# An MLP's first half: product down with weights loaded anew for each factor, attention running on beside it

## The chip, the core and the metric

The kernel runs on one core of a Trainium2 chip. Time is device microseconds of one launch; lower is better. Engines: PE (matmul) with PEld (its weight loads), DVE, ACT, POOL, and SP, which issues most DMAs.

## What is computed

One layer on x, 2048 tokens by 1024. All is float32 outside; inside, each float32 matrix is split into a high and a low float16 part, and a product takes three matmuls (high x high, low x high, high x low).

```python
h = rmsnorm(x); proj = h @ w_in            # three head groups read h
y_a = s5_mixer(...)                        # state-space scan
y_b = diff_attention(dq, dk, dv, ...)      # 6 heads, two softmax maps each
y_c = hgrn2_mixer(cq, cf, ci, cg, ...)     # gated linear recurrence
x = x + concat(y_a, y_b, y_c) @ w_out
h = rmsnorm(x)
up = causal_conv3(h @ w_up) + conv_b; gate = h @ w_gate     # 1024 -> 2816
x = x + (gelu(up) * gate) @ w_down                          # 2816 -> 1024
return rmsnorm(x)
```

Attention, per head and block of 128 queries: scores of two maps over all keys up to the block's end, softmax of each, `w = p0 - lam * p1`, `o = w @ v`.

## The kernel before, in words

**Two streams woven.** The program is written by two generators. `fore` (`left`) writes the input projection and then attention: first query blocks 0 to 7 of all heads, then blocks 8 to 15 of all heads. The other (`right`) writes the state-space part, the recurrence, and then `phase_tail`: output projection and MLP. Each yields a number, its cost; `weave` goes on with the stream whose sum is smaller. The cost of a block of attention is its number of key blocks times a weight of the list `LW`: `LW[4]` for blocks 8 to 15. A larger weight lets attention advance more slowly beside the tail. Within the order so written, a scheduler sets the order of each engine when the kernel is built; on the chip each engine runs its instructions strictly in that order.

**The tail.** Tokens 0 to 1023 are the first half, the rest the second. `first` projects the first half (`o_pm`), normalises it, and runs 22 *up tiles* (`tile_of`, one for each 128 columns of the 2816; 84 matmuls `f_pm` each); half of these also make the float16 weights `f_w`, the other half load them. Each ends in conv, GELU and the factors `f_a`, which go to the DRAM tensors `Ad`. Then comes the *product down* of the first half (`Down`): a Strassen scheme with seven products, numbered 0 to 6, of 132 matmuls `f_pd` each. Product i multiplies a left factor `f_da` (loaded from `Ad`) by a right factor `f_dw`, which is the split of a quarter of `w_down` or of a difference of quarters. The sums go onto the rows `f_r` (loaded from `Xd`) in `put`, on DVE. Then `second` does the output projection of the second half, with product 6 inside it; the second half's up tiles and its product down end the kernel, with no attention beside them.

**Attention beside it.** For each block: scores `t_ps` (chunks of 512 keys), which DVE moves with bias and running maximum to `t_sc` (L839); exponent on ACT (L849); the difference of the maps on DVE (L861); per 512 keys four transposes `t_pt`, two copies on ACT, the low part `t_wt` on POOL (L875), and twelve matmuls `t_po` per four key blocks. After eight blocks of a head pair: a chain of thirteen tiny DVE operations for the norm, a scaling on POOL (L903), transposes of `t_y` (L910) and the split `t_yo` to `Yd`.

**Right factors before.** A right factor has four cuts of 3, 3, 3 and 2 row blocks, and `f_dw` has six buffers, so that two cuts of the next product can be written while four are in use. For products 0 to 3 the quarters are streamed through three buffers `f_dst` of at most two row blocks (`stage`), the difference made by POOL in place, the split by ACT (high) and DVE (low, L62). Ahead of product 2, `before()` writes out all of attention that is left, because the 88 KB a partition that hold the four raw quarters `f_db` (`hold`, `load`) lie where attention's buffers were. Products 4 to 6 take their differences from `f_db`, by POOL, one operation of 128x1536 or 128x1024 a cut. The second half's product down uses the same class with all quarters held.

Of the kernel before, what the change touches and what calls it, by code (L numbers as in the profile page):

```python
# [9 lines left out]
F32 = mybir.dt.float32  # L10
# [4 lines left out]
ALU = mybir.AluOpType  # L15
# [7 lines left out]
MF = DFF // 128  # L23
# [3 lines left out]
CH = 512  # L27
# [8 lines left out]
MADE = range(0, MF, 2)  # L36
LW = [6.0, 0.44, 5.0, 2.5, 0.62, 1.0]

# [1289 lines left out]
def phase_tail(K, x, Xd, Yd, Ad, w_out, norm_g, W, conv_w, conv_b, w_down, final_g, out, es,  # L1328
# [228 lines left out]
    class Down:  # L1557
# [18 lines left out]

        LOADS = ({2: (B12, B11), 3: (B22,), 4: (B21,)}, {0: (B21,), 1: (B22, B11), 2: (B12,)})

# [20 lines left out]

        def stage(self, i, st, cs=(0, 1, 2, 3)):  # L1600

            for c in cs:
                q0, n = self.cuts[c]
                w = self.room(i, c)
                for q in range(0, n, 2):
                    k = min(2, n - q)
                    b, pair, _ = self.STEPS[i]
                    fs = []
                    for b in pair or (b,):
                        f = st.tile([128, KD, 128], F32, tag="wst", name="f_dst")  # L1610
                        f = f.rearrange("p (q a) f -> p q (a f)", q=2)[:, 0:k]
                        nc.sync.dma_start(out=f, in_=self.source(b, q0 + q, k))
                        fs.append(f)
                    f = fs[0]
                    if pair:
                        add(f, f, fs[1], ALU.subtract, P)
                    K.split(w[:, 0, q:q + k], w[:, 1, q:q + k], f, WS)

# [89 lines left out]

        def run(self, rs, tp, pms, side, staged, before):


            self.rs, self.tp = rs, tp
            with ExitStack() as e1:
                pool = pooler(e1)
                st = pool("f_dst", 3) if staged > 1 else None
                self.more(pool)
                if not self.w:
                    self.ahead(st)
                with ExitStack() as e2:
                    for i in range(6):  # L1720
                        for c in range(len(self.cuts)):
                            if (i, c) not in self.a:
                                self.left(i, c)
                        if i == staged - 1 - (staged > 1):
                            before()
                            self.hold(pooler(e2)("f_db", 1, side))
                        for b in self.LOADS[self.half].get(i, ()):
                            self.load(b)
                        if i + 1 < staged:
                            self.stage(i + 1, st)  # L1730
                        else:
                            for c in range(len(self.cuts)):
                                if i + 1 == staged == 4:
                                    self.sum(3, c)
                                self.right(i + 1, c)
                        if i < 5:
                            yield from self.product(i, pms[i % len(pms)], False)
                yield from self.product(5, pms[5 % len(pms)], False)
                if self.half == 1:
                    yield from self.product(6, pms[6 % len(pms)], True)  # L1740
            self.last = self.product(6, pms[0], False)

# [146 lines left out]
    with ExitStack() as e2:  # L1889
# [6 lines left out]
        down = Down(0, pooler(el))  # L1896
        yield from down.run(total(0), tp, [pm], "left", 4, ahead)
        eh = ExitStack()
# [7 lines left out]
    eh.close()  # L1906
    yield from down.run(total(1), tp, [pd, pm], "left", 1, lambda: None)

# [116 lines left out]
```

## Time and profile before

| what | value |
|---|---|
| time, median of 3 runs | 2810.27 us (2809.77 to 2811.77) |
| profiled execution | 2806.09 us, span 2804.4 us |
| PE / DVE / ACT / POOL busy | 90% / 72% / 48% / 48% of the span |
| first up matmul, first f_pd | 1225.1 us, 1869.8 us from the span's start |
| last t_po | 1932.7 us |
| next output projection (o_pm) | from 2062.5 us |
| second half's up tiles | from 2195.7 us |

A page of the profile gives busy time by engine, slices of the span, the chain that ended last and the costliest groups of instructions. Rows of groups read: line, engine, operation, out<-in, count, busy time, mean ns of one, idle time of the engine before them and what ended it. Rows of the timeline read: start, length, engine, line, operation, and in brackets the idle time before it and who ended it. Matmuls are pipelined: a run of them shows their pace, a single one its latency.

### The profile page before, as it was taken

How to read it: one execution, taken by the hardware profiler on the slowest of the kernel's cores; microseconds unless marked ns; L12 is line 12 of the kernel's file. 1: busy time of each engine (PE TensorE's matmuls, PEld its weight loads, DVE VectorE, ACT ScalarE, POOL GpSimd, SP SyncE). 2: the span in 40 equal slices, each digit the busy share in tenths (PEclk: the TensorE clock that was granted, in tenths of full speed). 3: DMA queues.
4: the chain of work that ended last, by engine and by line, in shares of the span. 5: the costliest groups of instructions: out<-in, count | busy, mean ns of one | idle time of the engine just before them, and what ended most of it. 6: DMA issues, size and time to landing. Idle time of an engine off the chain costs nothing.

```text
span 2804.4 us, 44619 instructions
## 1 busy us (share of the span) xinstructions
PE 2528.7 (90%) x16254; PEld 1465.3 (52%) x16254; DVE 2008.0 (72%) x3904; ACT 1341.1 (48%) x2579; POOL 1347.2 (48%) x1191
## 2 busy tenths in 40 slices
PE   5998898989999998968898888879999999999998
PEld 3654546877777765444444444434444444444443
DVE  7566745788787887798888889885654855555565
ACT  5333344557665665676565456653134422222221
POOL 4788602334343443266566666642801444444180
PEclk8999998989989989989999999989999999999999
DMA  6675553232223225623444434357775655554733
GB/s 225 234 219 187 166 169 99 65 91 69 60 78 91 52 86 134 211 84 112 135 135 128 152 111 128 101 213 242 270 264 197 215 166 155 166 154 143 267 105 120
DMA packets 339500, 420.74 MB, mean 150 GB/s; under 512 B 61840, under 2 KB 217808, under 8 KB 338256
## 3 DMA queue, kind: packets, MB, share of 16 engines
q1 hardware_dynamic: 317104, 377.51, 42.8%
q10 hardware_dynamic: 22176, 40.38, 3.9%
q8 instruction: 128, 2.10, 0.3%
q14 instruction: 92, 0.75, 0.1%
HBM read 289.30 MB, written 127.93 MB: 149 GB/s over the span
## 4 chain that ended last, share of the span: by engine, by line
PE 41%; DVE 16%; issue 6%; ACT 4%; DMA 4%; POOL 4%; SPq 0%; ACTq 0%; DVEq 0%; POOLq 0%
PE f_pm L98 18%; PE f_pd L1679 10%; DVE t_sc L839 3%; PE o_pm L1394 3%; DVE t_sc L861 2%; PE g_pv L98 2%; PE g_pq L98 1%; ACT t_sc L849 1%; PE t_pt L871 1%; DVE f_t L1520 1%; PE t_ps L835 1%; DVE f_w L62 1%; DMA o_y<-Yd 1%; PE g_pl L1147 1%; PE t_po L883 1%
## 5 line engine op out<-in xcount | busy, mean ns | idle before, releaser
L98 PE MATMUL f_pm<-f_q,f_w 128*128 128x512 f16 x3696 | 857.8, 388 | 6.2 <-DVE rs_i L72 5.7
L98 PEld LDWEIGHTS <-f_w 128*128 128x128 f16 x3696 | 365.3, 100 | 493.7 <-issue 98.4
L875 POOL TENSOR_TENSOR t_wt<-t_wf,t_wt 128x512 f16<-128x512 f32 (+2 forms) x240 | 286.5, 1195 | 451.3 <-ACT t_wt L874 365.0
L1679 PE MATMUL f_pd<-f_dw,f_da 128*128 128x512 f16 x1848 | 406.9, 382 | 9.5 <-DMA f_da<-Ad 7.8
L1679 PEld LDWEIGHTS <-f_da 128*128 128x128 f16 x1848 | 181.3, 98 | 228.7 <-DMA f_da<-Ad 8.8
L849 ACT ACTIVATE t_sc<-t_sc,t_nm 128x128 f32<-128x128 f32 (+7 forms) x192 | 229.2, 1198 | 53.5 <-DVE t_nm L844 51.9
L835 PE MATMUL t_ps<-t_k,t_q 96*128 96x512 f16 (+2 forms) x480 | 170.0, 369 | 83.7 <-DVE t_mx L839 80.5
L839 DVE CUSTOM_DVE_ANT_0 t_sc<-t_ps,t_base,t_mx 128x512 f32<-128x512 f32 (+3 forms) x288 | 185.2, 643 | 36.4 <-PE t_ps L835 29.6
L873 ACT ACTIVATE t_wf<-t_pt 128x512 f32<-128x512 f32 (+2 forms) x240 | 126.7, 528 | 132.9 <-PE t_pt L871 96.1
L883 PE MATMUL t_po<-t_v,t_wt 128*128 128x64 f16 x2448 | 145.5, 198 | 37.1 <-POOL t_wt L875 32.4
L883 PEld LDWEIGHTS <-t_wt 128*128 128x128 f16 x2448 | 124.8, 101 | 94.3 <-POOL t_wt L875 48.0
L861 DVE SCALAR_TENSOR_TENSOR t_sc<-t_sc,t_a 128x1024 f32<-128x1024 f32 (+7 forms) x144 | 167.9, 1193 | 1.6
L98 PE MATMUL g_pq<-g_h,g_w 128*128 128x256 f16 x1152 | 157.3, 291 | 9.9 <-DVE g_sg L1069 7.3
L60 DVE TENSOR_TENSOR f_a<-f_t,f_a 128x512 f16<-128x512 f32 x132 | 134.8, 1027 | 39.6 <-ACT f_a L54 36.1
L98 PE MATMUL g_pv<-g_w,g_h 128*128 128x256 f16 x1152 | 151.1, 284 | 12.0 <-ACT g_w L54 8.0
L1744 POOL TENSOR_TENSOR f_k<-f_k,f_k 128x512 f32<-128x512 f32 x88 | 126.1, 1433 | 73.1 <-ACT f_k L1776 65.9
L871 PE MATMUL t_pt<-ident,t_sc 128*128 128x128 f32 x816 | 146.6, 296 | 14.6 <-ACT t_wt L874 9.4
L1744 POOL TENSOR_TENSOR f_db<-f_db 128x1536 f32<-128x1536 f32 (+1 forms) x32 | 129.2, 4073 | 61.0 <-DMA f_db<-in_w_down_dram 61.0
L1744 POOL TENSOR_TENSOR f_t<-f_t,f_t 128x512 f32<-128x512 f32 x66 | 104.3, 1594 | 108.5 <-ACT f_a L54 85.4
L1394 PE MATMUL o_pm<-o_w,o_y 128*128 128x512 f16 x624 | 145.0, 388 | 10.0 <-DMA o_y<-Yd 9.6
L54 ACT ACTIVATE f_a<-f_t 128x512 f16<-128x512 f32 x154 | 95.9, 629 | 118.1 <-POOL f_t L1744 54.9
L62 DVE SCALAR_TENSOR_TENSOR f_dw<-f_db,f_dw 128x1536 f16<-128x1536 f32 (+1 forms) x36 | 104.0, 2904 | 55.2 <-ACT f_dw L54 55.2
(328 smaller groups left out, 4856.5 us busy)
## 6 DMA issues: line engine op xcount, KB each, us to landing
f_w<-Wd SPq DMA_DIRECT2D x231, 256.0 KB, 2.7
Wd<-f_w SPq DMA_DIRECT2D x154, 256.0 KB, 2.1
Ad<-f_a ACTq DMA_DIRECT2D x154, 256.0 KB, 2.3
f_da<-Ad SPq DMA_DIRECT2D x42, 768.0 KB, 4.5
g_h<-Hd SPq DMA_DIRECT2D x24, 1024.0 KB, 6.5
f_db<-in_w_down_dram SPq DMA_DIRECT2D x24, 768.0 KB, 8.7
o_wst<-in_w_out_dram SPq DMA_DIRECT2D x32, 512.0 KB, 5.8
o_y<-Yd SPq DMA_DIRECT2D x52, 256.0 KB, 4.9
```

What stands on the lines that cost most here:

```text
L60: nc.vector.tensor_tensor(out=lo, in0=src, in1=hi, op=ALU.subtract)
L98: nc.tensor.matmul(out=out, lhsT=lhs(a, k), rhs=rhs(b, k), start=(n == 0), stop=(n == 3 * nk - 1))
L835: nc.tensor.matmul(out=ps[:, 0:k1 - k0], lhsT=qt[:, c, 128 * (i % 4):128 * (i % 4) + 128], rhs=kt[:, c, k0:k1], start=True, stop=True,)
L839: V.tensor_tensor_reduce(out=sc[c][:, k0:k1], in0=ps[:, 0:k1 - k0], in1=bs[:, k0:k1], scale=1.0, scalar=-3e38 if j == 0 else mx[:, c, j - ...
L849: nc.scalar.activation(out=sc[c][:, 0:L], in_=sc[c][:, 0:L], func=AF.Exp, scale=SLOPES[h], bias=nm[:, c:c + 1], accum_out=la[:, c, n_:n_ + 1],
L861: V.scalar_tensor_tensor(out=sc[0][:, k0:k1], in0=sc[1][:, k0:k1], scalar=a[:, 1:2], in1=sc[0][:, k0:k1], op0=ALU.mult, op1=ALU.add,)
L871: nc.tensor.transpose(pt[:, b:b + 128], sc[0][:, k + b:k + b + 128], K.ident)
L875: nc.gpsimd.tensor_tensor(out=wt[:, 1, 0:n], in0=wf[:, 0:n], in1=wt[:, 0, 0:n], op=ALU.subtract)
L883: nc.tensor.matmul(out=po, lhsT=wts[b // 4][:, w, cc], rhs=vt[:, b, 64 * v:64 * v + 64], start=(b == 0 and w + v == 0), stop=(b == i and w ...
L1394: nc.tensor.matmul(out=ps[t], lhsT=y[:, k, a, 128 * t:128 * t + 128], rhs=w[:, b, k, :], start=(q == qs[0] and i == 0), stop=(q == qs[-1] ...
L1679: nc.tensor.matmul(out=ps[t], lhsT=a[:, q, x, tk], rhs=w[:, y, q, :], start=(first and q + x + y == 0), stop=(last and q == n - 1 and y == 1),
L1744: eng.tensor_tensor(out=o, in0=a, in1=b, op=op)
```

## The change

The product down of the first half gets a method of its own, `streamed`. Each of its right factors is loaded anew from `w_down` through `f_dst` (now four buffers): one quarter for products 0, 1, 2 and 6, two for 3 and 4, three for 5. The sum for product 5 is kept in a single tile `f_db` (22 KB a partition), and product 6 subtracts the quarter B21 from it. `f_db` again lies where attention's buffers were, but it is opened only ahead of product 4, so `before()` stands there. `LW[4]` rises from 0.62 to 0.72. The second half's product down loses only the options it did not use.

```diff
-LW = [6.0, 0.44, 5.0, 2.5, 0.62, 1.0]
+LW = [6.0, 0.44, 5.0, 2.5, 0.72, 1.0]
...
-        LOADS = ({2: (B12, B11), 3: (B22,), 4: (B21,)}, {0: (B21,), 1: (B22, B11), 2: (B12,)})
+        LOADS = {0: (B21,), 1: (B22, B11), 2: (B12,)}
...
+        SUMS = (
+            (B11,), (B21,), (B22,), (B12, B11), (B22, B12), (B22, B12, B11), (B21,),
+        )
+
+        def stage(self, i, st, kept=None):
+            for c, (q0, n) in enumerate(self.cuts):
                 w = self.room(i, c)
                 for q in range(0, n, 2):
                     k = min(2, n - q)
                     fs = []
+                    for b in self.SUMS[i]:
                         f = st.tile([128, KD, 128], F32, tag="wst", name="f_dst")
                         f = f.rearrange("p (q a) f -> p q (a f)", q=2)[:, 0:k]
                         nc.sync.dma_start(out=f, in_=self.source(b, q0 + q, k))
                         fs.append(f)
                     f = fs[0]
+                    if i == 6:
+                        add(f, kept[:, q0 + q:q0 + q + k], f, ALU.subtract, P)
+                    elif len(fs) > 1:
                         add(f, f, fs[1], ALU.subtract, P)
+                    if i == 5:
+                        t = kept[:, q0 + q:q0 + q + k]
+                        add(t, f, fs[2])
+                        f = t
                     K.split(w[:, 0, q:q + k], w[:, 1, q:q + k], f, WS)
...
+        def streamed(self, rs, tp, pm, before):
+            self.rs, self.tp = rs, tp
+            with ExitStack() as e1:
+                pool = pooler(e1)
+                st = pool("f_dst", 4)
+                self.more(pool)
+                self.ahead(st)
+                kept = None
+                for i in range(6):
+                    for c in range(len(self.cuts)):
+                        if (i, c) not in self.a:
+                            self.left(i, c)
+                    if i == 4:
+                        before()
+                        kept = e1.enter_context(
+                            tc.tile_pool(name="f_db", bufs=1, side="left", reuse_waits="tile")
+                        ).tile([128, MF // 2, CH], F32, name="f_db")
+                    self.stage(i + 1, st, kept)
+                    yield from self.product(i, pm, False)
+            self.last = self.product(6, pm, False)
...
-        yield from down.run(total(0), tp, [pm], "left", 4, ahead)
+        yield from down.streamed(total(0), tp, pm, ahead)
```

All engines keep their order up to the first up tile, and again from the second output projection's middle on. Between them, counted in the order of instructions (t_po on PE, score chunks L839 on DVE):

| | before | after |
|---|---|---|
| t_po among the up tiles / up to the first f_pd / behind it | 917 / 62 / 93 | 706 / 117 / 249 |
| score chunks on DVE from the first to the last up sum (f_k from f_pm) / up to the first sum of f_pd / behind it | 158 / 11 / 0 | 117 / 23 / 30 |
| f_pd ahead of the last attention instruction on PE | 311 | 660 |
| f_pd ahead of the next o_pm on PE | 792 | 696 |

*SP, at the passage from the up tiles to the product down* (`Wd_106<-f_w` stores up weights; `f_dst` are quarters of w_down, `f_r` the rows, `f_da` left factors). Before:

```order
L145 DMA Wd_106<-f_w 128x1024 x7
L1612 DMA f_dst<-in_w_down_dram 128x2x512
L1612 DMA f_dst<-in_w_down_dram 128x512
L1612 DMA f_dst<-in_w_down_dram 128x2x512
L1885 DMA f_r<-Xd 128x1024 x8
L1650 DMA f_da<-Ad_70 128x3072 x2
```

After:

```order
L145 DMA Wd_106<-f_w 128x1024 x2
L1907 DMA f_r<-Xd 128x1024 x8
L1660 DMA f_da<-Ad_70 128x3072 x2
L1616 DMA f_dst<-in_w_down_dram 128x2x512
L1616 DMA f_dst<-in_w_down_dram 128x512
L1616 DMA f_dst<-in_w_down_dram 128x2x512
```

The first three loads of w_down have moved behind the rows and the first two left factors.

*PE, at the last attention instruction* (transposes of `t_y`). Before, within product 2:

```order
L1679 LDWEIGHTS f_da
L1679 MATMUL f_pd<-f_dw,f_da 128x512
L910 MATMUL t_pt<-ident,t_y 128x128 x4
L1679 LDWEIGHTS f_da
L1679 MATMUL f_pd<-f_dw,f_da 128x512
```

After, between products 4 and 5:

```order
L883 LDWEIGHTS t_wt
L883 MATMUL t_po<-t_v,t_wt 128x64
L910 MATMUL t_pt<-ident,t_y 128x128 x8
L1689 LDWEIGHTS f_da
L1689 MATMUL f_pd<-f_dw,f_da 128x512
```

No f_pd stands any more between the last t_po and the transposes, nor between the two groups of transposes.

*DVE, at the same place* (L902 ends the norm's chain, `t_yo` is attention's last output, `f_dw` the right factors' low parts). Before:

```order
L902 TENSOR_TENSOR t_e_21987<-t_e_21987,rs_y 128x8
L1657 SCALAR_TENSOR_TENSOR f_r<-f_pd,f_r 128x512 x3
L62 SCALAR_TENSOR_TENSOR f_dw<-f_dst,f_dw 128x1024
L62 SCALAR_TENSOR_TENSOR t_yo<-t_pt,t_gc,t_yo 128x512
L62 SCALAR_TENSOR_TENSOR f_dw<-f_dst,f_dw 128x512
L62 SCALAR_TENSOR_TENSOR t_yo<-t_pt,t_gc,t_yo 128x512
L62 SCALAR_TENSOR_TENSOR f_dw<-f_dst,f_dw 128x1024
```

After:

```order
L902 TENSOR_TENSOR t_e_22669<-t_e_22669,rs_y 128x8
L62 SCALAR_TENSOR_TENSOR t_yo<-t_pt,t_gc,t_yo 128x512 x2
L1766 TENSOR_TENSOR f_db<-f_dst 128x1024
L1766 TENSOR_TENSOR f_db<-f_dst 128x512
L62 SCALAR_TENSOR_TENSOR f_dw<-f_db,f_dw 128x1024
L62 SCALAR_TENSOR_TENSOR f_dw<-f_db,f_dw 128x512
L1766 TENSOR_TENSOR f_db<-f_dst 128x1024
```

The weights of product 5 (`f_dw<-f_db`) are made only behind attention's last output.

More of the change, by code (lines that the diff above doesn't have):

```diff
@@ L1598, in room @@
             return w
-        def stage(self, i, st, cs=(0, 1, 2, 3)):
-            for c in cs:
-                q0, n = self.cuts[c]
+        SUMS = (
[3 more added lines that the diff above has]
+            for c, (q0, n) in enumerate(self.cuts):
                 w = self.room(i, c)
@@ L1606, in stage @@
                     k = min(2, n - q)
-                    b, pair, _ = self.STEPS[i]
                     fs = []
-                    for b in pair or (b,):
+                    for b in self.SUMS[i]:
                         f = st.tile([128, KD, 128], F32, tag="wst", name="f_dst")
@@ L1707, in product @@
                 yield 2.5 * self.cuts[c][1]
-        def run(self, rs, tp, pms, side, staged, before):
+        def streamed(self, rs, tp, pm, before):
             self.rs, self.tp = rs, tp
@@ L1714, in run @@
                 pool = pooler(e1)
-                st = pool("f_dst", 3) if staged > 1 else None
+                st = pool("f_dst", 4)
                 self.more(pool)
-                if not self.w:
-                    self.ahead(st)
+                self.ahead(st)
[12 more added lines that the diff above has]
+            self.last = self.product(6, pm, False)
+        def run(self, rs, tp, pms, side):
+            self.rs, self.tp = rs, tp
+            with ExitStack() as e1:
+                pool = pooler(e1)
+                self.more(pool)
                 with ExitStack() as e2:
@@ L1723, in run @@
                                 self.left(i, c)
-                        if i == staged - 1 - (staged > 1):
-                            before()
+                        if i == 0:
                             self.hold(pooler(e2)("f_db", 1, side))
-                        for b in self.LOADS[self.half].get(i, ()):
+                        for b in self.LOADS.get(i, ()):
                             self.load(b)
[L1729 to L1735, printed above, removed]
+                        for c in range(len(self.cuts)):
+                            self.right(i + 1, c)
                         if i < 5:
@@ L1738, in run @@
                 yield from self.product(5, pms[5 % len(pms)], False)
-                if self.half == 1:
-                    yield from self.product(6, pms[6 % len(pms)], True)
-            self.last = self.product(6, pms[0], False)
+                yield from self.product(6, pms[6 % len(pms)], True)
     def add(o, a, b, op=ALU.add, eng=V):
@@ L1906, in phase_tail @@
     eh.close()
-    yield from down.run(total(1), tp, [pd, pm], "left", 1, lambda: None)
+    yield from down.run(total(1), tp, [pd, pm], "left")
 @with_exitstack
```

1 line of the change is left out of this document (removed).

## The prediction

> **What bounds the kernel now.** I read the page first: its span, the busy shares and the slices.
>
> ```profile
> span 2804.4 us, 44619 instructions
> PE 2528.7 (90%) x16254; PEld 1465.3 (52%) x16254; DVE 2008.0 (72%) x3904; ACT 1341.1 (48%) x2579; POOL 1347.2 (48%) x1191
> PE   5998898989999998968898888879999999999998
> PEclk8999998989989989989999999989999999999999
> ```
>
> PE is busy in 90% of the span, but unevenly: the weak slices lie in the middle, where attention runs beside the MLP. So I cut the span at what PE runs (tables of busy time by stretch): the 22 up tiles of the first half with attention beside them, the passage to the first product down, that product's six parts up to the second output projection, and, for comparison, the up tiles of the second half, which have no attention.
>
> ```profile
> 1225.00:1846.00 621.00, 539.39 (x3244) 269.32 (x3243) 543.09 (x853) 375.11 (x676) 403.34 (x284) 0.93 0.38 122
> 1846.00:1870.00 24.00, 13.90 (x94) 7.87 (x93) 21.74 (x38) 15.89 (x27) 15.05 (x12) 0.62 0.68 253
> 1870.00:2062.50 192.50, 182.98 (x925) 85.76 (x924) 117.38 (x120) 60.88 (x89) 91.44 (x34) 0.98 0.69 242
> 2195.70:2600.00 404.30, 404.30 (x1864) 182.82 (x1864) 233.64 (x312) 118.00 (x218) 185.05 (x140) 0.99 0.53 162
> ```
>
> Columns: stretch, length, then busy time of PE, PEld, DVE, ACT, POOL, granted clock, DMA share, GB/s. The same 22 tiles take 404 us without attention and 621 us with it. With it DVE and PE are both at 87%; in the passage DVE is at 91% and PE at 58%, at a granted clock of 0.62; beside the product down PE is at 95% and DVE only at 61%. Who waits in the up tiles (waits of PE there):
>
> ```profile
> PE t_ps L835 <- DVE t_mx L839: 50.7, 30, 4.6
> PE t_po L883 <- POOL t_wt L875: 22.0, 20, 5.8
> ```
>
> Nearly all of PE's 82 us of idle time there is PE standing at an attention matmul whose input or bank DVE or POOL has not released. The up matmuls behind it in PE's queue wait too.
>
> **The change, part by part.** Attention does not get shorter; a part of it moves. From the order of instructions: of the 1072 t_po matmuls behind the first up matmul, 917 stand among the up tiles, 62 in the passage and 93 among the product's; after the change 706, 117 and 249. Of the score chunks that DVE takes (L839), between the first and the last addition of an up product 158 become 117, from there to the first f_pd sum 11 become 23, behind it none become 30.
>
> *Price of a chunk on DVE.* The DVE groups of 1225 to 1846:
>
> ```profile
> L839 DVE CUSTOM_DVE_ANT_0 t_sc<-t_ps,t_base,t_mx 128x512 f32<-128x512 f32 (+3 forms) x119 | 78.8, 662 | 6.5 <-PE t_ps L835 3.8 <-DVE t_mx L839 0.5
> L861 DVE SCALAR_TENSOR_TENSOR t_sc<-t_sc,t_a 128x1024 f32<-128x1024 f32 (+7 forms) x49 | 65.9, 1384 | 0.4
> L839 DVE CUSTOM_DVE_ANT_0 t_sc<-t_ps,t_base 128x512 f32<-128x512 f32 x48 | 32.6, 679 | 1.8 <-PE t_ps L835 1.4 <-PE t_pt L871 0.4
> L844 DVE SCALAR_TENSOR_TENSOR t_nm<-t_mx,t_lk 128x2 f32<-128x2 f32 x24 | 15.0, 626 | 0.2
> L839 DVE DVE_READ_ACCUMULATOR2_ANT t_mx<- 128x1 f32 x167 | 13.1, 79 | 0.0
> L855 DVE TENSOR_SCALAR t_a<-t_la,t_a,t_nlam 128x1 f32<-128x1 f32 x25 | 6.7, 270 | 0.4
> L854 DVE RECIPROCAL t_a<-t_la 128x1 f32<-128x1 f32 x24 | 3.9, 161 | 29.3 <-ACT t_sc L849 29.3
> ```
>
> Together 216.0 us for 167 chunks, 1.29 us each. *Price on PE.* From the timeline of PE, where the product down covers everything: four transposes and twelve t_po take 1915.22 - 1914.44 = 0.78 us, one score matmul 0.22 us (1834.89 - 1834.67).
>
> ```profile
> 1834.67 0.38 PE L835 MATMUL t_ps<-t_k,t_q 96*128 96x512 f16 x1
> 1834.89 4.26 PE L98 MATMUL f_pm<-f_q,f_w 128*128 128x512 f16 x19
> 1914.44 0.60 PE L871 MATMUL t_pt<-ident,t_sc 128*128 128x128 f32 x4
> 1914.88 0.51 PE L883 MATMUL t_po<-t_v,t_wt 128*128 128x64 f16 x12
> 1915.22 5.13 PE L1679 MATMUL f_pd<-f_dw,f_da 128*128 128x512 f16 x23
> ```
>
> (a) *Up tiles.* 41 chunks leave. If DVE sets the time at its present share, 41 x 1.29 / 0.875 = 60 us go; if PE did, 211 t_po (17.6 groups of twelve) x 0.78 + 41 x 0.22 = 23 us. PE's waits on DVE and POOL above put it near the first: -55. Bounds -23 and -61.
>
> (b) *Passage.* 12 chunks more, and nothing else on PE: 12 x 1.29 / 0.906 = +17. Lower bound at PE's price (55 t_po): 6. SP now issues the eight f_r loads ahead of the first f_dst loads, which before stood ahead of them; the longer passage covers that.
>
> (c) *Products 0 to 4.* 156 t_po and 31 score matmuls arrive: 13 x 0.78 + 31 x 0.22 = +17 at PE's price, since DVE has 75 us free there. The upper bound is DVE's price, 30 x 1.29 = 39.
>
> (d) *The end of attention.* Before, the last row's tail ran under f_pd (timeline, one f_dw split among it):
>
> ```profile
> 1932.40 0.46 PE L883 MATMUL t_po<-t_v,t_wt 128*128 128x64 f16 x10
> 1932.69 11.17 PE L1679 MATMUL f_pd<-f_dw,f_da 128*128 128x512 f16 x51
> 1943.70 0.60 PE L910 MATMUL t_pt<-ident,t_y 128*128 128x128 f32 x4
> 1944.13 6.42 PE L1679 MATMUL f_pd<-f_dw,f_da 128*128 128x512 f16 x29
> 1946.02 1.06 ACT L54 ACTIVATE f_dw<-f_dst 128x1024 f16<-128x1024 f32 x1 [3.58 <-POOL f_dst L1744]
> 1947.11 1.23 DVE L62 SCALAR_TENSOR_TENSOR f_dw<-f_dst,f_dw 128x1024 f16<-128x1024 f32 x1 [5.50 <-ACT f_dw L54]
> 1950.39 0.60 PE L910 MATMUL t_pt<-ident,t_y 128*128 128x128 f32 x4
> ```
>
> Now the last three groups and both transposes of t_y stand behind the last matmul of product 4 and ahead of the first of product 5, and on DVE and ACT the first sum for product 5's weights (into the new f_db) stands behind both t_yo. The cover is gone. From last t_po to first transpose it was 11.0 us, of which DVE's small chain and POOL are the need and about half was other DVE work; to the second transpose 6.7, about half of it need; the first sum and its split on ACT and on DVE (two of the three are the f_dw rows above, the sum taken as long as the DVE one) 1.06 + 1.23 + 1.23 = 3.5; the uncovered groups about 3. I take 7.5 + 3.5 + 4 + 3 = +18; bounds 11 (the need alone) and 25.
>
> (e) *Weights.* The raw quarters go. Two of PE's waits before go with the burst of loads and POOL sums they brought:
>
> ```profile
> 1981.20 31.21 PE L1679 MATMUL f_pd<-f_dw,f_da 128*128 128x512 f16 x136 [4.10 <-DMA f_da<-Ad]
> 2014.13 11.17 PE L1679 MATMUL f_pd<-f_dw,f_da 128*128 128x512 f16 x51 [1.72 <-DVE f_r L1657]
> ```
>
> -4 (bounds -6 and 0). Eleven quarter loads replace nine: 5.8 MB more, on a queue that moved 242 GB/s here. POOL's sums and the one sum per piece on DVE lie under f_pd (DVE 61%, POOL 48% busy); if that cover fails it is rival 2. The f_da loads keep their order behind f_dst loads on SP, so a late sum holds them too; that is counted there. The 46 o_pm matmuls which now stand between the parts of product 5 are moved, not added: 0.
>
> Sum: -55 + 17 + 17 + 18 - 4 = -7 us. The profiled execution took 2806.1 us (1.7 outside its span), 4.2 under the median 2810.3 of the three runs; so 2799 for such a run, and 2803 against the median. A change within 0.2% (5.6 us) counts as none here.
>
> **Where the skill bears on it.** In the up tiles the two-input operation L60 takes 1128 ns on average, where its shortest takes 674:
>
> ```profile
> L60 DVE TENSOR_TENSOR f_a<-f_t,f_a 128x512 f16<-128x512 f32 x61 | 68.3, 1128 | 6.6 <-ACT f_a L54 6.6
> L60 DVE TENSOR_TENSOR f_a<-f_t,f_a x132: 674/792/1758, 1295.5 to 2606.6; 128x512 f16<-128x512 f32 x132
> ```
>
> The Trainium skill (GPSIMD Engine Reference, Specifications) says that GpSimd shares its SBUF interfaces with VectorE, which contend when a DVE instruction has two SBUF inputs. By that rule POOL's part of the moved attention also stops stretching what stays, and (a) would end at its far bound, -61; the trace agrees as to L60 but does not show the slope, so this stays in rival 3.
>
> **Rivals.**
> 1. *The up tiles give less (slower).* PE stands at 87% there too; its matmuls and DVE's operations interlock, and with less attention PE may set the pace in some tiles. Halfway between the bounds of (a), -38, the sum is +10: 2820. It decides once (a) falls short of 42. For it: both engines at 87%. Against: PE's waits.
> 2. *Product 5's weights come late.* Only two of its seven pieces can be loaded before attention ends, since three of the four f_dst buffers go to one piece. Five pieces (three full, two half) then pass one after another:
>
> ```profile
> f_dst<-in_w_down_dram SPq DMA_DIRECT2D x17, 512.0 KB, 4.9
> f_dst<-in_w_down_dram SPq DMA_DIRECT2D x12, 256.0 KB, 3.7
> 1943.63 2.35 POOL L1744 TENSOR_TENSOR f_dst<-f_dst 128x1024 f32<-128x1024 f32 x1 [2.63 <-DMA f_dst<-in_w_down_dram]
> ```
>
> With the splits of (d), a full piece takes 4.9 + 2.35 + 1.23 + 1.06 + 1.23 = 10.8, a half one about 7: 46 us in series, against PE's 178 matmuls (132 f_pd, 46 o_pm) at 5.13/23 = 0.223 us, 40 us. That is 6 to 10 us late with the first piece's own delay: 2811. Against it: loads of one piece overlap the sums of another, which I take as likelier. The Trainium skill (DMA: Bandwidth & Descriptors, Bandwidth) lists 0.95 us for 64 KB and 6.15 us for 1 MB; an estimate between the two for 512 KB is 3.4 us where the row has 4.9, and by that the five pieces would take about 40 us and this rival would vanish. The row decides.
> 3. *More comes free (faster).* (a) at -61, (e) at -6, 2 us off (d): -15 to -20, about 2792.
>
> **Chances.** Forecast (2790 to 2811 by itself) 0.45, of that 0.31 faster and 0.14 same; rival 1 0.24 (0.02 same, 0.22 slower); rival 2 0.18 (half same, half slower); rival 3 0.13. So faster 0.44, same 0.25, slower 0.31. The range 2780 to 2824 reaches past rivals 1 and 3 by what (b) to (d) leave open; all upper bounds at once (-23 + 17 + 39 + 25) would be +58, which I leave out.
>
> **What would show it.** (a): from first up matmul to last, 565 us instead of 621, DVE still near 87%. (b): the passage near 41 us, filled with t_sc on DVE. (c): products 1 to 4 at 31 to 38 us each, without long waits of t_ps on DVE. (d): one gap of 15 to 20 us on PE just ahead of product 5, ended by f_dw's split. (e): no wait on f_da near 4 us. Wrong if the up tiles keep over 580 us, if the gap ahead of product 5 exceeds 30, or if PE waits within product 5 for f_dw.

## Result and the profile after

The changed kernel is slower: median 2840.8 us (2837.4 to 2845.7) against 2810.0 us (2808.5 to 2811.8) for the kernel before, ratio 1.011, 95% interval 1.009 to 1.013. Its profiled execution took 2842.4 us with a span of 2840.7, against 2806.1 and 2804.4 before: 36.3 us more, of which 4.7 lie ahead of the first up matmul, where the order of work has not changed; in the kernels below that leave attention's work as it is, that matmul starts between 1222.8 and 1232.7.

The same cut as in the prediction, by stretches of the trace of after (length, then busy time of PE, PEld, DVE, ACT, POOL, granted clock, DMA share, GB/s): up tiles; passage; products 0 to 4; the gap ahead of product 5; product 5; the rest up to the second half's first up matmul.

```profile
1229.80:1824.00 594.20, 513.94 (x2946) 250.96 (x2945) 488.77 (x731) 327.59 (x594) 383.76 (x268) 0.94 0.38 125
1824.00:1860.60 36.60, 23.12 (x155) 13.53 (x154) 31.44 (x81) 24.42 (x45) 19.36 (x15) 0.55 0.58 216
1860.60:2032.50 171.90, 166.00 (x960) 82.08 (x959) 103.64 (x169) 68.82 (x118) 54.93 (x35) 0.98 0.61 211
2032.50:2053.30 20.80, 7.39 (x73) 5.13 (x71) 6.99 (x21) 6.95 (x15) 5.67 (x5) 0.67 0.33 102
2053.30:2097.00 43.70, 41.80 (x183) 18.18 (x183) 23.37 (x18) 10.85 (x13) 20.44 (x9) 0.96 0.89 311
2097.00:2232.00 135.00, 115.87 (x535) 54.20 (x534) 80.45 (x145) 62.22 (x115) 34.43 (x23) 0.94 0.63 228
```

And of before, cut at the same events (its first up matmul is at 1225.1; there is no gap ahead of product 5):

```profile
1225.10:1848.30 623.20, 541.56 (x3255) 270.20 (x3252) 545.29 (x854) 375.64 (x676) 405.64 (x285) 0.93 0.38 123
1848.30:1869.80 21.50, 11.43 (x81) 6.78 (x82) 19.44 (x37) 15.06 (x25) 12.75 (x11) 0.58 0.65 242
1869.80:2033.20 163.40, 153.88 (x790) 72.62 (x789) 102.22 (x103) 53.06 (x78) 87.14 (x33) 0.97 0.71 250
2033.20:2061.40 28.20, 28.20 (x133) 12.76 (x132) 14.06 (x16) 7.33 (x10) 4.30 (x2) 1.00 0.62 205
2061.40:2195.70 134.30, 121.98 (x587) 58.12 (x586) 75.67 (x142) 60.52 (x110) 27.25 (x19) 0.98 0.66 231
```

In the up tiles (623.2 us, after 594.2) DVE has 56.5 us less to do, but the stretch is only 29.0 shorter. PE's busy time fell by 27.6 and its idle time stayed, 81.6 before and 80.3 after; DVE is now at 82% there. The stages behind give more than that back: passage +15.1, products 0 to 4 +8.5, the gap +20.8, product 5 +15.5, the rest +0.7 (46 o_pm matmuls, 10 us, have moved from the rest into product 5, so both belong together: +16).

The passage has a wait on SP's queue that before does not have: the first f_dst loads, product 0's weights, stand 22.9 us until DVE has made a factor f_a of the up tiles (L60). The waits of SP's queue, after (us in total, times, longest):

```profile
SPq L1616 <- DVE f_a L60: 22.9, 1, 22.9
```

and its timeline:

```profile
1829.34 0.91 SPq L1660 DMA_DIRECT2D f_da<-Ad  x2
1853.23 2.19 SPq L1616 DMA_DIRECT2D f_dst<-in_w_down_dram  x4
```

The gap, on PE's timeline after: the last groups of attention and the two transposes of t_y with nothing beside them, then the first split of product 5's weights.

```profile
2040.29 0.71 PE L883 MATMUL t_po<-t_v,t_wt 128*128 128x64 f16 x10 [1.05 <-POOL t_wt L875]
2045.53 1.12 PE L910 MATMUL t_pt<-ident,t_y 128*128 128x128 f32 x4 [4.52 <-POOL t_y L903]
2048.21 1.11 PE L910 MATMUL t_pt<-ident,t_y 128*128 128x128 f32 x4 [1.56 <-DVE t_yo L62]
2053.29 9.50 PE L1689 MATMUL f_pd<-f_dw,f_da 128*128 128x512 f16 x36 [3.97 <-ACT f_dw L54]
```

Behind it PE waits 15.9 us for o_y, the second projection's input (6.6 before); the waits of PE after, from the first f_pd to the second half:

```profile
PE o_pm L1394 <- DMA o_y<-Yd: 15.9, 6, 4.6
```

and before:

```profile
PE o_pm L1394 <- DMA o_y<-Yd: 6.6, 5, 2.9
```

### The profile page after: what moved, and what is told of

Read it like the earlier page. It is cut to its first block, busy times and chain, and to the rows that moved or that the text cites. A ratio compares the mean times of both kernels' runs of the same rounds, so it can differ in the third digit from the quotient of the medians.

```text
span 2840.7 us, 44727 instructions
## 1 busy us (share of the span) xinstructions
PE 2537.4 (89%) x16254; PEld 1468.4 (52%) x16254; DVE 1986.4 (70%) x3920; ACT 1331.7 (47%) x2580; POOL 1326.7 (47%) x1196
## 4 chain that ended last, share of the span: by engine, by line
PE 39%; DVE 16%; issue 6%; ACT 6%; DMA 4%; POOL 4%; SPq 0%; ACTq 0%; DVEq 0%; POOLq 0%
PE f_pm L98 15%; PE f_pd L1689 11%; DVE t_sc L839 3%; PE o_pm L1394 2%; ACT t_sc L849 2%; DVE t_sc L861 2%; DMA f_dst<-in_w_down_dram 2%; PE g_pv L98 2%; DVE f_a L60 1%; PE g_pq L98 1%; PE t_pt L871 1%; DVE f_t L1520 1%; PE t_ps L835 1%; DVE f_w L62 1%; POOL f_k L1766 1%
## 5 line engine op out<-in xcount | busy, mean ns | idle before, releaser
L1689 PE MATMUL f_pd<-f_dw,f_da 128*128 128x512 f16 x1848 | 413.2, 382 | 6.3 <-ACT f_dw L54 5.0
L1689 PEld LDWEIGHTS <-f_da 128*128 128x128 f16 x1848 | 180.6, 98 | 221.9 <-issue 15.1
L839 DVE CUSTOM_DVE_ANT_0 t_sc<-t_ps,t_base,t_mx 128x512 f32<-128x512 f32 (+3 forms) x288 | 185.3, 644 | 49.0 <-PE t_ps L835 41.1
L60 DVE TENSOR_TENSOR f_a<-f_t,f_a 128x512 f16<-128x512 f32 x132 | 137.5, 1049 | 49.7 <-ACT f_a L54 45.7
L871 PE MATMUL t_pt<-ident,t_sc 128*128 128x128 f32 x816 | 148.3, 299 | 20.2 <-DVE t_sc L861 11.3
L1394 PE MATMUL o_pm<-o_w,o_y 128*128 128x512 f16 x624 | 149.3, 395 | 18.9 <-DMA o_y<-Yd 18.4
L1766 POOL TENSOR_TENSOR f_k<-f_k,f_k 128x512 f32<-128x512 f32 x88 | 125.6, 1427 | 75.6 <-ACT f_k L1798 66.9
L1813 ACT ACTIVATE f_t<-f_t,f_cb 128x1024 f32<-128x1024 f32 x44 | 50.5, 1148 | 211.3 <-DVE f_t L1520 211.2
L839 DVE CUSTOM_DVE_ANT_0 t_sc<-t_ps,t_base 128x512 f32<-128x512 f32 (+2 forms) x192 | 120.8, 632 | 31.9 <-PE t_ps L835 24.1
```

What stands on the lines that cost most here:

```text
L60: nc.vector.tensor_tensor(out=lo, in0=src, in1=hi, op=ALU.subtract)
L839: V.tensor_tensor_reduce(out=sc[c][:, k0:k1], in0=ps[:, 0:k1 - k0], in1=bs[:, k0:k1], scale=1.0, scalar=-3e38 if j == 0 else mx[:, c, j - ...
L871: nc.tensor.transpose(pt[:, b:b + 128], sc[0][:, k + b:k + b + 128], K.ident)
L1394: nc.tensor.matmul(out=ps[t], lhsT=y[:, k, a, 128 * t:128 * t + 128], rhs=w[:, b, k, :], start=(q == qs[0] and i == 0), stop=(q == qs[-1] ...
L1689: nc.tensor.matmul(out=ps[t], lhsT=a[:, q, x, tk], rhs=w[:, y, q, :], start=(first and q + x + y == 0), stop=(last and q == n - 1 and y == 1),
L1766: eng.tensor_tensor(out=o, in0=a, in1=b, op=op)
```

## Experiments

Theory 1: moving attention out of the up tiles saves there what PE had to do for it, and costs more behind them. Theory 2 (the prediction's): DVE sets the up tiles, so the loss must lie in the streamed weights. To compare, I cut every trace in three. U: from the first up matmul to the last. A: from there to the end of attention (the last transpose of t_y), less the f_pd matmuls that the order puts ahead of that end, at 0.217 us each (22.39 us for 103 in a row quoted below). R: from there to the second half's first up matmul, less the other f_pd of the 924 likewise. So A is what attention costs PE behind the up tiles, waits and all, and R is projection, loads and waits. Each is read from one profiled execution. The ratios are those to executions of before made beside each kernel, with medians of 2807.7 to 2812.7 us.

| kernel | weights of products 0 to 6 | pace | median us | ratio (95%) | U | A | R |
|---|---|---|---|---|---|---|---|
| before | 4 streamed, 3 held | 0.62 | 2810.0 | 1 | 623.2 | 35.2 | 111.7 |
| after | 7 streamed, 4 buffers | 0.72 | 2840.8 | 1.009 to 1.013 | 594.5 | 81.8 | 123.9 |
| e1 | 7 streamed, 4 buffers | 0.62 | 2839.2 | 1.008 to 1.012 | 625.3 | 48.4 | 122.5 |
| e2 | 4 streamed, 3 held | 0.72 | 2866.5 | 1.017 to 1.023 | 595.7 | 84.3 | 145.2 |
| e5 | 7 streamed, 3 buffers | 0.72 | 2850.9 | 1.011 to 1.016 | 594.2 | 82.7 | 131.9 |
| e6 | 7 streamed, 3 buffers | 0.62 | 2837.6 | 1.006 to 1.012 | 623.9 | 35.3 | 139.0 |
| e7 | 7 streamed, 3 + 3 buffers | 0.72 | 2844.0 | 1.009 to 1.013 | 594.7 | 77.7 | 133.4 |
| e8 | e5, six rows of f_db early | 0.72 | 2859.6 | 1.014 to 1.020 | 594.2 | 83.7 | 138.6 |
| e9 | e6 without product 6's loads | 0.62 | 2823.3 | 1.003 to 1.005 | 625.3 | 35.3 | 125.3 |
| e10 | e6, loads on ACT's queue | 0.62 | 2839.5 | 1.007 to 1.012 | 625.4 | 35.3 | 138.7 |
| e11 | 4 streamed, 3 held | 0.66 | 2840.4 | 1.008 to 1.013 | 591.2 | 62.5 | 149.2 |
| e12, 0.66 | 5 streamed, 2 held | 0.66 | 2811.5 | 0.999 to 1.001 | 591.9 | 54.3 | 125.8 |
| e12, 0.64 | 5 streamed, 2 held | 0.64 | 2822.7 | 1.002 to 1.006 | 604.3 | 43.8 | 133.6 |
| e13 | 4 streamed, 3 held | 0.64 | 2812.5 | 0.999 to 1.001 | 604.5 | 41.2 | 127.1 |
| e14, one part | e12, a part of product 5 streamed | 0.66 | 2823.6 | 1.004 to 1.007 | 589.8 | 55.7 | 132.0 |
| e14, two parts | e12, two parts of it streamed | 0.66 | 2833.1 | 1.008 to 1.011 | 590.1 | 56.0 | 147.6 |

**Each half of the change alone.** e1 is after with the pace back, e2 is before with the new pace.

```
e1 (on after):  LW = [6.0, 0.44, 5.0, 2.5, 0.62, 1.0]
e2 (on before): LW = [6.0, 0.44, 5.0, 2.5, 0.72, 1.0]
```

> The changed kernel with the old pace of attention, 0.62: only the streaming of the weights is left of the change. The loss of 30 us is shared out differently by three theories. (A) The pace is to blame: attention's share moved out of the up tiles saved only 29 us there and cost 44 (passage +15, products 0 to 4 +8.5, gap ahead of product 5 +21), so without the pace this kernel is within 4 us of the one before, 2806 to 2814. (B) The streamed weights are to blame: product 5 late (+4) and the second projection's o_y loads late (+9 of waits) stay, and the up tiles are back at 621 to 625: 2820 to 2830. (C) Both: the gap needs attention to end late and weights to need its room; then no gap is seen ahead of product 5, and the time is 2818 to 2826 from the late loads alone.

> The kernel before with the new pace, 0.72: only the pace is left of the change, the four quarters are held in attention's room and loaded once it is free. Up tiles 590 to 600 us in every theory (as in the changed kernel). (A) Pace to blame: passage about 36, products 0 to 4 about 10 over before, and one gap of 20 to 40 us where the held quarters wait for attention's room: 2835 to 2850. (B) Streaming to blame: no more than the passage and the products' +10 on the bad side, no waits on o_y over 8 us in the second projection: 2800 to 2812.

Both halves lose: streaming by 1.0%, the pace by 2.0%, both together 1.1%. All three theories for e1 were too low: it has no gap, but a passage of 41.9 us, with the same wait of SP as after, 29.7 us long. In e2 the up tiles fall as in after, the passage is back at 22.0 us, and product 4 stands 32.8 us for its held quarters, which need attention's room; with the tail ahead of it that is more than the 20 to 40 us of theory A, and the time, 2866.5 us, is above the ranges of both theories. Waits of SP's queue in e1:

```profile
SPq L1616 <- POOL f_a L58: 29.7, 1, 29.7
```

The passage of e1, as a stretch:

```profile
1856.90:1898.80 41.90, 19.88 (x145) 12.94 (x146) 27.23 (x54) 24.57 (x43) 21.59 (x17) 0.54 0.38 135
```

The passage of e2:

```profile
1824.30:1846.30 22.00, 10.50 (x75) 6.50 (x74) 21.76 (x42) 16.22 (x25) 10.21 (x8) 0.58 0.93 372
```

Waits of PE behind it in e2:

```profile
PE f_pd L1679 <- ACT f_dw L54: 32.8, 1, 32.8
```

So the passage's +15 comes with the new weights, not with the pace: e1, at the old pace, has the longest passage, and DVE is busy in only 27.2 us of it. The up tiles' -29 is a matter of the pace.

**What sets the up tiles.** Two edits of the kernel before, in the rows 8 to 15 of attention only. e3 leaves out the difference of the two maps, so its result is not that of the layer. Each ran once and is read for its up tiles alone.

```diff
 e3: less work on DVE (L861)
-for k0 in range(0, L, 1024):
+for k0 in range(0, L if i0 == 0 else 0, 1024):
 e4: more work on PE (t_po)
-for w, v in ((0, 0), (0, 1), (1, 0)):
+terms = ((0, 0), (0, 1), (1, 0)) * (2 if i0 else 1)
+for n, (w, v) in enumerate(terms):
```

> The kernel before without the combination of the two score maps (the DVE operation of line 861, in the rows 8 to 15): 66 us of DVE work leave the up tiles, and the order moves a few chunks of attention out of them too (178 score matmuls become 168, worth 7 us of PE and 9 of DVE). If DVE sets the up tiles (the prediction's price, 1.29 us a chunk over 0.875), they fall from 623 to 535 to 555 us. If PE's own work and its fixed waits set them, they stay at 600 to 616 and PE's idle time there keeps 70 to 85 us.

> The kernel before with each t_po product of the rows 8 to 15 done twice: the order then has 2026 instead of 979 t_po among the up tiles, 1047 more at 0.059 us, +62 us of PE work and no work for DVE, POOL or ACT. If PE's own work sets the up tiles, they grow by 50 to 62 us, to 673 to 685, with PE's idle time unchanged. If DVE sets them, the new matmuls go into PE's 82 us of idle time and they grow by at most 25, to 648.

The up tiles of e3:

```profile
1224.00:1805.90 581.90, 520.19 (x3159) 259.61 (x3158) 451.28 (x783) 361.69 (x655) 385.87 (x282) 0.96 0.40 131
```

The up tiles of e4:

```profile
1236.20:1889.90 653.70, 567.11 (x4289) 301.48 (x4288) 548.85 (x881) 385.04 (x699) 415.17 (x293) 0.96 0.37 121
```

A group of doubled t_po on PE's timeline of e4:

```profile
1917.05 0.86 PE L884 MATMUL t_po<-t_v,t_wt 128*128 128x64 f16 x24
1917.75 2.54 PE L1680 MATMUL f_pd<-f_dw,f_da 128*128 128x512 f16 x11
```

My expectation for e4 had the price wrong: 24 t_po take 0.70 us (1917.75 - 1917.05), 0.029 each, so 1047 more are 30.5 us. The up tiles grew by 30.5, which lies between the two theories; that it equals the price is chance, for PE's busy time grew by 25.5 and its idle time by 5.0, at a granted clock of 0.96 instead of 0.93. In e3 DVE lost 94.0 us of busy time and the up tiles 41.3, neither theory's value: 21.4 of that is PE's busy time, 19.9 is idle time gone, again at 0.96.

So the clock has to be taken out. In the up tiles the traces grant PE either the full clock or half of it; f_pm in a row start 0.427 us apart in the half stretches and 0.216 us elsewhere. PE's work at full clock, an estimate, is its busy time with the part in the half stretches counted half; what that takes off is lost to the clock. In us (e11 and e13 are described below):

| kernel | pace | U | PE's work at full clock | lost to the clock | idle |
|---|---|---|---|---|---|
| before | 0.62 | 623.2 | 506.5 | 35.1 | 81.6 |
| e13 | 0.64 | 604.5 | 502.9 | 24.7 | 76.9 |
| e11 | 0.66 | 591.2 | 497.2 | 18.4 | 75.6 |
| after | 0.72 | 594.5 | 484.1 | 30.2 | 80.3 |
| e2 | 0.72 | 595.7 | 484.6 | 27.5 | 83.6 |
| e3 | 0.62 | 581.9 | 500.9 | 19.3 | 61.7 |
| e4 | 0.62 | 653.7 | 542.3 | 24.8 | 86.6 |

The other kernels agree with the one of their pace within 1 us in the work, 3 in the clock's loss and 3 in the idle time. In e4 PE's work grew by 35.8 and none of it went into idle time; the clock gave 10.3 back. In e3 PE's work fell by 5.6; DVE's 94 us brought 19.9 of idle time and 15.8 of clock, together less than half their length. From before to after PE's own work fell by 22.4, the clock's loss by 4.9 and the idle time by 1.3.

**The wait for room in the passage.** e5 is after with three buffers, e6 the same at pace 0.62.

```diff
-st = pool("f_dst", 4)
+st = pool("f_dst", 3)
```

> The changed kernel with three buffers for the raw weight pieces (f_dst) instead of four, as before the change. Theory R (room): the fourth buffer lies in room that the up tiles' factors hold to the end, so the first f_dst load waited 22.9 us on f_a and the first matmul of product 0 came late; with three buffers the loads go out ahead of the f_r loads, the passage falls from 36 us to 20 to 24, and the time by 10 to 16, to 2824 to 2832; the gap ahead of product 5 stays at 18 to 30. Rival (the prediction's): the passage is long because attention's chunks that stand in it take DVE's time; then it stays at 34 to 38 and the time within 4 us of the changed kernel.

> Streamed weights at the old pace of 0.62, with three f_dst buffers: the streaming alone, without the wait for room. Theory R: of the 27 us that streaming at the old pace lost, the passage's 20 go: 2815 to 2823, with a passage of 20 to 24 us; what stays are waits on f_r at the starts of products 3 to 5, where the second projection's first matmuls now stand. If the streaming costs by its loads and sums (18 pieces more on SP and POOL), the loss only moves to products 1 to 5 and the time stays at 2830 to 2842.

The fourth buffer is shown to be the cause: with three the loads go out ahead of f_r and the passage is 22.4 us in e5 and 21.5 in e6. With three, though, the order also puts less of attention into it (75 matmuls on PE in e5, 155 in after), so the two kernels do not separate the wait from these chunks; e1's passage, long with DVE at 27.2 of 41.9 us, speaks for the wait. SP's timeline of e5:

```profile
1818.30 1.42 SPq L1616 DMA_DIRECT2D f_dst<-in_w_down_dram  x3
1819.81 9.34 SPq L1907 DMA_DIRECT2D f_r<-Xd  x8
```

Its passage, as a stretch:

```profile
1824.20:1846.60 22.40, 10.47 (x75) 6.50 (x74) 22.16 (x42) 16.32 (x25) 10.27 (x8) 0.57 0.91 367
```

But the time I expected from it did not come. In e5 attention's end stays where it was, 2050.1 against 2049.3, and A is unchanged at 82.7: the products start 14 us earlier and then stand more, since product 5 cannot start ahead of that end. R rises by 8, and e5 is 10 us slower than after, above both of its ranges. In e6, where attention ends early, A falls by 13 against e1, to the value of before, and R rises by 16.5: the loss has moved, as its second case said. The wait was real, and its removal shortened neither kernel beyond the noise.

**More buffers, other room.** e7 puts three more f_dst buffers behind the other pools; e8 takes e5 and gives six of the eleven rows of f_db room of their own.

```diff
 e7 (excerpt)
+st = [st, pool("f_dsu", 3)]             # used in turn
 e8 (excerpt)
+early = pool("f_dc", 1).tile([128, 6, CH], F32, name="f_dc")
-kept = ... .tile([128, MF // 2, CH], F32, name="f_db")
+late = ... .tile([128, MF // 2 - 6, CH], F32, name="f_db")
```

> The changed kernel with six buffers for the raw pieces: three as in the kernel before and three in room of their own behind the others, used in turn. Theory R: passage 20 to 24 us as with three buffers; if too few buffers also made product 5's weights and the second projection's o_y loads late, product 5 falls from 43.7 (46 o_pm in it) to about 29 to 33 without the o_pm and the waits on o_y from 16 to 6 to 10 us: 2810 to 2820 in all. If those come from attention's late end alone, the gap ahead of product 5 and the o_y waits stay: 2822 to 2832.

> The kernel with three f_dst buffers, and six of the eleven rows of the kept sum (f_db) in room of their own, so that the weights of product 5's first two parts need not wait for attention's room. If the gap ahead of product 5 comes from that room (theory of the prediction's term d): the gap falls from 20 to 0 to 8 us, and the time to 2806 to 2816. If it comes from attention's last tail on DVE, POOL and ACT, whatever room is used, it stays at 15 to 22 us and the time at 2824 to 2832.

e7 has the gap of its second case (A stays at 77.7), but its time, 2844.0 us, is above both ranges: o_pm waits for o_w (15.2 us) as well as o_y (10.2), with 19 f_dst loads now going out in one row ahead of the projection's. e8, too, is above both of its ranges. The order now puts 72 f_pd of product 5 ahead of attention's end, which comes 17 us later for it, and the same bare tail follows, ahead of the first part of product 5 that needs attention's room. PE's timeline of e8:

```profile
2058.39 0.47 PE L883 MATMUL t_po<-t_v,t_wt 128*128 128x64 f16 x10 [1.05 <-POOL t_wt L875]
2063.39 1.11 PE L910 MATMUL t_pt<-ident,t_y 128*128 128x128 f32 x4 [4.53 <-POOL t_y L903]
2066.07 1.11 PE L910 MATMUL t_pt<-ident,t_y 128*128 128x128 f32 x4 [1.56 <-DVE t_yo L62]
2071.15 10.86 PE L1689 MATMUL f_pd<-f_dw,f_da 128*128 128x512 f16 x36 [3.97 <-ACT f_dw L54]
```

**What streaming costs in R.** On e6, whose U and A are those of before. e9 leaves out product 6's loads and the subtractions of B21, so its result is not that of the layer.

```diff
 e9: product 6 from the kept sum alone (excerpt)
-for b in self.SUMS[i]:
+for b in self.SUMS[i] if i < 6 else ():
 e10: another queue
-nc.sync.dma_start(out=f, in_=self.source(b, q0 + q, k))
+queue = nc.scalar if i >= 5 else nc.sync
+queue.dma_start(out=f, in_=self.source(b, q0 + q, k))
```

> Streamed weights, pace 0.62, three buffers (2837.6 us), without the six raw loads of product 6's weights and their subtractions: product 6's right factor is made from the kept sum alone. Theory Q (SP's queue): these loads stand on SP ahead of the second projection's o_y and o_w loads and each waits there for a buffer that a split of product 5 or 6 must free, so the projection starves; without them the waits of o_pm on o_y fall from 18.8 us to 5 to 9 and the time to 2821 to 2829. Rival (the product's own work: splits, sums and f_r additions): the waits stay at 15 to 20 and the time at 2833 to 2841.

> Streamed weights, pace 0.62, three buffers, with the raw loads of the products 5 and 6 issued on ACT's queue instead of SP's, the same bytes to the same buffers. Theory Q: o_y and o_w loads no longer stand behind them, the waits on o_y fall from 18.8 to 5 to 10 us, and the time to 2820 to 2830, less what ACT loses by standing at loads that wait for a buffer. If the bytes moved in that stretch are the cause (DMA 0.83 to 0.89 busy), o_y comes as late as before and the time stays at 2833 to 2842.

Waits of PE on o_y in e6:

```profile
PE o_pm L1394 <- DMA o_y<-Yd: 18.8, 6, 6.1
```

in e9:

```profile
PE o_pm L1394 <- DMA o_y<-Yd: 8.7, 4, 3.3
```

and in e10:

```profile
PE o_pm L1394 <- DMA o_y<-Yd: 15.2, 6, 6.7
```

Without product 6's loads and subtractions the o_y waits fall by 10 us and the median by 14, half of what streaming at the old pace costs; so these loads, or the subtractions on POOL behind them, delay the projection. That it is their place on SP's queue is not shown: from ACT's queue they cost the same. The Trainium skill (DMA: Bandwidth & Descriptors, "Issuing engines are not separate DMA queues") says that DMAs started by different engines end up on the same 16 DMA engines and interleave there, so that a second issuing engine saves issue time alone. e10 agrees, 2839.5 us against 2837.6.

**The pace, with the held quarters needed later.** e11 and e13 are before at 0.66 and 0.64. In e12 product 4 is streamed as well, and products 5 and 6 use held quarters.

```diff
 e11 (on before): pace 0.66; e13 (on before): pace 0.64
-LW = [6.0, 0.44, 5.0, 2.5, 0.62, 1.0]
+LW = [6.0, 0.44, 5.0, 2.5, 0.66, 1.0]
 e12 (on before), besides the pace
-LOADS = ({2: (B12, B11), 3: (B22,), 4: (B21,)}, ...
+LOADS = ({3: (B12, B11, B22), 4: (B21,)}, ...
-yield from down.run(total(0), tp, [pm], "left", 4, ahead)
+yield from down.run(total(0), tp, [pm], "left", 5, ahead)
```

> The kernel before with a pace of 0.66: less of the pace, held quarters. 103 t_po and 22 score matmuls leave the up tiles. At PE's price (8.6 groups of twelve at 0.78 and 22 at 0.22) they fall by 11 us, at the prediction's price on DVE (22 chunks at 1.29 over 0.875) by 32. Behind them attention ends some 25 to 40 us later than at 0.62, and the held quarters' loads with it, so that product 4 waits 0 to 15 us. PE's price: 2804 to 2820. DVE's price: 2785 to 2800.

> The kernel before, its held quarters unchanged, at a pace of 0.64: 42 t_po leave the up tiles. If the up tiles' 32 us at 0.66 came from what stands first (tiles 1 to 4) they fall by 10 to 25 here already; attention ends 5 to 15 us later than at 0.62 against the products, and product 4 waits 0 to 12 us: 2800 to 2815. At PE's own price, 5 us, and no gap: 2806 to 2813.

> Between the two kernels: product 4's weights are streamed too, but those of the products 5 and 6 come from quarters held in attention's room as before the change; pace 0.66. At that pace the kernel with four streamed products gained 32 us in the up tiles and lost 41 at product 4, which stood 32.8 us for held quarters. If the room, needed too early, is what made the faster pace lose: the wait moves to product 5 and shrinks to 5 to 20 us, no late o_y, and the time is 2798 to 2815. If attention beside the products costs what it saves in the up tiles whatever the weights do: 2815 to 2835.

> The same with five streamed products at a pace of 0.64: attention ends during product 2 or 3, its room is free 20 us or more before product 5 needs its quarters, so no gap. If the room was the loss: up tiles 600 to 615, no wait over 6 us at products 4 and 5, 2793 to 2808. Otherwise 2810 to 2825.

At 0.66 the up tiles fell by 32 us, the prediction's price on DVE to the microsecond. That is chance: by the table above 9.3 of it is PE's work, 16.7 the clock and 6.0 idle time; and at 0.72, with about twice as much attention gone, they are no shorter. The up tiles of e13, at 0.64:

```profile
1226.30:1830.70 604.40, 527.48 (x3169) 263.47 (x3166) 521.56 (x832) 363.50 (x657) 389.20 (x281) 0.95 0.39 128
```

and of e11, at 0.66:

```profile
1232.30:1823.50 591.20, 515.60 (x3108) 257.03 (x3107) 507.64 (x806) 347.72 (x637) 398.37 (x280) 0.96 0.40 128
```

By the order, 42, 103, 156 (after) and 207 (e2) t_po fewer than before stand between the first up matmul and the first f_pd; U falls by 19, 32, 29 and 28. The saving stops near 30. PE's work goes on falling, by 3.6, 9.3, 22.4 and 21.9, near the price on PE (5, 11 and 23 us for the first three); what the clock and the idle time gave at 0.66, 22.7 us, is down to 6.2 in after. No run shows why. A meanwhile rises by 6, 19 to 27, 47 and 49: it goes on. So U and A together gain 13 at 0.64 (e13) and 12 at 0.66 (e12), and lose 18 in after.

The times follow R. e11 stands 32.8 us at product 4, as e2 does, and both of its theories were too low. e13 stays within both of its ranges, its gain given back by a wait of 13.9 us for f_da behind the later burst of held loads (3.7 and 4.1 before). e12 at 0.66 is in its first range, equal to before; at 0.64 it is in its second, with 10.3 us of waiting for f_da and 11.3 for f_dw.

What e12 gains there goes in R. Its held quarters are loaded in one burst once attention's room is free, with the DMA engines full, and product 5 waits. That burst in e12 at 0.66, as a stretch:

```profile
1995.00:2030.00 35.00, 21.04 (x97) 9.33 (x95) 5.90 (x9) 1.48 (x1) 18.16 (x6) 0.87 1.02 364
```

PE's timeline there:

```profile
1992.92 22.39 PE L1679 MATMUL f_pd<-f_dw,f_da 128*128 128x512 f16 x103
2029.27 31.14 PE L1679 MATMUL f_pd<-f_dw,f_da 128*128 128x512 f16 x132 [13.96 <-ACT f_dw L54]
```

**Around that wait.** The last two kernels take e12 at 0.66 and make the first part, or the first two, of product 5's weights from newly loaded pieces:

```diff
 e14 (excerpt)
+if i + 1 == staged == 5 and c < 1:      # e14_part2: c < 2
+    self.streamed(c, st); continue      # B22 - B12 + B11 through f_dst
```

The held sums of that part, which product 6 needs, are made one product later.

> The kernel with five streamed products at pace 0.66 (2811.5 us, a wait of 14.0 us at product 5), with the first part of product 5's weights, three of its eleven rows, made from newly loaded pieces, which need no room of attention's. If that wait is the held quarters' loads behind attention's room: it falls to 4 to 9 us, as PE has 36 matmuls (8 us) for it and two more pieces per row to load, and the time to 2802 to 2810. If the pieces only delay the held quarters on the same queue, the wait moves behind part 1 and the time stays at 2809 to 2816.

> The same with the first two parts, six of eleven rows, from new pieces: 72 matmuls, 16 us of PE, in front of the held quarters. If the wait is the room: it falls to 0 to 5 us and the time to 2797 to 2808. If the twelve pieces delay the held quarters and the second projection's loads on SP: waits of 5 us and more at parts 1 or 3, o_y waits over 10 us, 2810 to 2822.

2823.6 us and 2833.1, each above even the worse of its two cases. The wait only moved, to the f_da loads behind the same burst, and in the second kernel to the held quarters too. Waits of PE with one part:

```profile
PE f_pd L1694 <- DMA f_da<-Ad: 12.2, 1, 12.2
```

and with two:

```profile
PE f_pd L1694 <- DMA f_da<-Ad: 18.9, 1, 18.9
PE f_pd L1694 <- ACT f_dw L54: 16.3, 1, 16.3
```

No kernel of this study that computes the layer beats the one before.

## Why the prediction was wrong

By U, A and R, after stands against before at -28.7, +46.6 and +12.2: +30.1, near the difference of the medians (30.8). The prediction had -55, +52 (b, c and d) and -4.

- **(a) Up tiles, -55, measured -29: the step that failed.** I took the price of a chunk on DVE because PE's waits named DVE and POOL, and multiplied it by the number of chunks. What left the up tiles was PE's own work: 22.4 us of it at full clock, the lower bound of (a), -23; a higher granted clock brought 4.9 and idle time only 1.3. It was the mechanism of rival 1, whose point of decision (42) was passed. (Halfway between the bounds of (a) is -42, not the -38 of rival 1; the forecast does not rest on it.) The waits of PE did not go with DVE's 56.5 us: those on t_mx fell (50.7 to 37.7 us), those on t_wt and t_sc rose (22.0 to 28.2, none to 4.7). After:

```profile
PE t_ps L835 <- DVE t_mx L839: 37.7, 29, 2.7
PE t_po L883 <- POOL t_wt L875: 28.2, 25, 3.9
PE t_pt L871 <- DVE t_sc L861: 4.7, 4, 2.5
```

PE's idle time there is between 73 and 84 us at each of the paces 0.62, 0.64, 0.66 and 0.72; with much less of DVE's work alone, in e3, it is 62. Why it keeps its size, and why the granted clock differs, is not settled; no run separates the order of PE's queue from the length of one row's chain. Rival 3 leaned on a rule of the Trainium skill (GPSIMD Engine Reference, Specifications), that GpSimd and VectorE contend for SBUF interfaces when a DVE instruction has two SBUF inputs. The traces are divided on it: POOL's busy time in the up tiles fell by 22 us, the two-input L60 takes 1182 ns where it took 1128, and the two-input L62 on f_w 971 ns where it took 1106. Groups of DVE in the up tiles, after:

```profile
L60 DVE TENSOR_TENSOR f_a<-f_t,f_a 128x512 f16<-128x512 f32 x62 | 72.5, 1182 | 16.1 <-ACT f_a L54 15.7
L62 DVE SCALAR_TENSOR_TENSOR f_w<-f_sum,f_w 128x512 f16<-128x512 f32 x54 | 52.2, 971 | 3.2 <-issue 1.6 <-ACT f_w L54 1.0 <-DMA Wd<-f_w 0.5
```

- **(b) Passage, +17, measured +15.1, for another reason.** I put it down to the pace, which moves attention's chunks there. The trace looks so (DVE has 12.0 us more to do in it), but e2, at that pace, has 22.0 us and e1, at the old one, 41.9; e5 shows that the fourth f_dst buffer made it. That the size came out is luck. I had even written that the f_r loads now go out ahead of the first f_dst loads, and taken that as covered. Removing the wait did not shorten the time, since attention's end sets the start of product 5.
- **(c) Products 0 to 4, +17 less the 4 of (e), measured +8.5.** Right in kind and 4.5 too high; no long wait of t_ps on DVE, as said. The f_da waits are gone, as (e) said.
- **(d) Gap ahead of product 5, +18, measured 20.8, at the place named and ended by f_dw's split.** Right. e8 adds that room for the first weights does not cover the tail: their 72 f_pd went ahead of it in the order, and not beside it.
- **(e) Weights, 0 beyond the f_da waits, measured +16 in product 5 and the projection.** The second step that failed. Product 5 without its o_pm took 5 us more. Rival 2 had put 6 to 10 there on late weights, but PE's waits for f_dw inside it are 1.8 us (1.00 and 0.75); a granted clock of 0.96 instead of 1.00 over its 43.7 us is about as much, and the rest is not traced. The projection waited 9 us more for o_y, which none of my cases had. I had called the 46 o_pm moved, not added, and looked at POOL and DVE for cover, not at what stands behind the loads. e6 prices streaming alone at 26 us at the old pace, and e9 puts 14 of them on product 6's loads and subtractions.

Together: (a) is 26 us off and (e), with its f_da waits, 16 by R. The range (2780 to 2824) left out the case of both.

## What to carry to other kernels

When work moves from one stage to another, price it in both stages on the engine that runs on, and take the price on the busier-looking partner as an upper bound: here -61 was the bound and -29 the result, while what the move costs behind was predicted well in sum. Compare busy times only with the granted clock beside them: more than half of the 32 us that 0.66 saved in the up tiles was clock. Before calling loads hidden, follow the queue past them to the next stage's first loads, and ask at what moment their room is free. And a long wait that one removes may be somebody else's cover: check first whether the work behind it can end any earlier.

## What the runs showed that was not expected

- The moved attention costs the same behind the up tiles however the weights are made: A is 77.7 to 84.3 us in all five kernels at 0.72 and 35.2 to 35.3 in before, e6, e9 and e10, where the first wait for room is absent.
- A t_po matmul (128 by 64) with a weight load of its own costs PE 0.029 us in a row of them, against 0.217 for an f_pd (128 by 512).
- Four quarters loaded in one burst behind attention (16 loads on SP's queue) fill the DMA engines for 35 us at 364 GB/s; in e12 product 5 then waits 14.0 us for its weights, and with streamed pieces added (e14) 12.2 and 18.9 us for f_da.
- The traces grant PE half the clock in 87 of the 623 us of up tiles before, in 72 of 595 after and in 43 of 591 in e11, and f_pm start there 0.427 us apart instead of 0.216.
